# Prompt heads of a differential attention: five score banks, and the second sub-head turned by a diagonal and added in PSUM

## The chip, the cores and the metric

The kernel runs on one core of one Trainium2 chip. What is measured is the device time of one execution in microseconds (us), as the median of several runs.

## The reference

One inference step of four layers: 0 = gated short convolution, 1 = a gated linear recurrence, 2 = differential attention, 3 = the convolution again. All in fp32, width 1024. The layers work on a prompt of 1024 tokens and on a sample group of 8 sequences with 4 new tokens each, whose 2048 earlier keys and values lie in pages of 128 rows. The change touches the attention of the prompt, in layer 2. It has 8 heads, each with two sub-heads of 64 query and key columns and one value of 128 columns:

```python
def diff_combine(p, lam):
    p = p.reshape(p.shape[0], N_HEADS, 2, p.shape[2], p.shape[3])
    return p[:, :, 0] - lam * p[:, :, 1]

# diff_attn_prompt, for a block of 128 queries:
sc = jnp.einsum('bqhd,bkhd->bhqk', qi, k).astype(jnp.float32)
sc = jnp.where(kpos[None, :] <= qpos[:, None], sc, -jnp.inf)
w = diff_combine(jax.nn.softmax(sc, axis=-1), lam).astype(v.dtype)
return jnp.einsum('bhqk,bkhd->bqhd', w, v)

# diff_attn_output:
of = of * lax.rsqrt(jnp.mean(jnp.square(of), axis=-1, keepdims=True) + SUBLN_EPS)
return (o * jax.nn.silu(z)) @ w_out
```

So a head's output is the difference of two softmaxes times the values, divided by its root mean square over 128 columns, gated, and projected by w_out.

## The kernel before, in words

Layer 2 runs as follows. The projections for queries, keys, values and gate come first (`qkv`, `zpath`); beside them the sample group's keys are read page by page and scored (`sample_keys`). Then `heads` works through the prompt's attention, and beside it `sample_values` reads 128 pages of values, 512 KB each, on SP's queue into five buffers, and multiplies each page by the sample group's probabilities (tile sacc, line 1524). Behind both the output projection starts (`boundary`, tile op, line 127).

`heads` goes over 64 blocks, 8 heads by 8 query blocks; block qb has (qb + 1) * 128 keys. A block passes through these steps, spread over three rounds of the loop, so that three blocks (`cur`, `old`, `older`) are in work at once:

- `score`: for each of the two sub-heads one or two chunks of up to 512 keys, two matmuls each, into a PSUM bank (tile S, line 1210). DVE finds the minimum (lines 1248 and 1250; scores have their sign turned, and the last chunk takes the mask with it).
- `expo`: ACT reads the bank, writes the probabilities P of the sub-head to SBUF and their sum to rr (line 1262).
- `combine`: DVE adds the sums of the two chunks (line 1279), takes reciprocals (1281), forms the factor -lambda * sum0 / sum1 in a column of rr (1282), and writes P0 + factor * P1 over P0 (1284, one instruction over all keys of the block).
- `turn`: PE transposes P0 in pieces of 128x128 into a bank (tile wtp, line 1293), and ACT copies the bank to SBUF (tile wt, line 1295).
- `apply`: PE multiplies the turned pieces by the values (tile pv, line 1303).
- `finish`: ACT scales by 1 / sum0 into O (line 1312), then squares O and sums the squares (tile sq, line 1314). After every fourth block `outputs` (DVE line 1217, GpSimd lines 1218 and 1220) divides four blocks by their root mean square, and `store` transposes them (ytp, 1226) and gates them (1229 to 1232).

PSUM has eight banks. In this stage three of them (tag R) hold scores, one each (Q and U) serve turns, pv and ytp in turn, and three (P) serve the sample group: sacc, and in `gather_o` the transposes of its result (tile sot, line 1553). A tile of a tag waits until the tile that had its bank before was read.

`chain` ties the order of DVE's instructions for minima and combine to the written order. All other order is a planner's: the program is written as one list, the values' pieces merged into the heads' by the costs that the generators `yield`, with the total `tot` and a factor `ahead` of 1.1 (the values are to be done when the heads are at 1 / 1.1 of their cost); the heads' instructions get a priority of 50 places; and a simulation with its own durations decides the order on each engine. An engine then works strictly in that order.

Of the kernel before, what the change touches and what calls it, by code (L numbers as in the profile page):

```python
# [10 lines left out]
F32 = mybir.dt.float32  # L11
# [3 lines left out]
AF = mybir.ActivationFunctionType  # L15
ALU = mybir.AluOpType
AX = mybir.AxisListType
PSUM = bass.MemoryType.PSUM
# [28 lines left out]
class Trunk:  # L47
# [30 lines left out]

    def bank(self, kind, name):
        tag = next(self.deals[kind])  # L80
        pool = self.psb if tag in "PQ" else self.psum
        return pool.tile([128, 512], F32, tag=tag, bufs=self.BANKS[tag], name=name)

    def tp(self, name):
# [1086 lines left out]
    def heads(self, y):  # L1171
        nc = self.nc
        ident = self.ident
        lo_, hi_ = slice(0, 64), slice(64, 128)
        halves = ((lo_, hi_), (hi_, lo_))
        ks, V, sz, qs, O, ss = {}, {}, {}, {}, {}, {}
# [93 lines left out]
        def chain(inst):  # L1270
            if last:
                self.after(inst, last.pop())
            last.append(inst)

        def combine(x):
            qb, P, rr = x["qb"], x["P"], x["rr"]
            N = (qb + 1) * 128
            if N > 512:
                chain(nc.vector.tensor_reduce(
                    rr[:, 0:2], rr[:, 16:20].rearrange("p (s i) -> p s i", s=2), axis=AX.X, op=ALU.add))  # L1280
            chain(nc.vector.reciprocal(rr[:, 4:6], rr[:, 0:2]))
            chain(nc.vector.scalar_tensor_tensor(
                rr[:, 10:11], rr[:, 0:1], rr[:, 5:6], self.nlam, ALU.mult, ALU.mult))
            chain(nc.vector.scalar_tensor_tensor(
                P[0][:, :N], P[1][:, :N], rr[:, 10:11], P[0][:, :N], ALU.mult, ALU.add))

        def turn(x):
            h, qb, P = x["h"], x["qb"], x["P"]
            x["w"] = []
            for o, w in chunks(qb):  # L1290
                wp = self.tp(f"wtp{h}_{qb}_{o}")
                for j in range(0, w, 128):
                    nc.tensor.transpose(wp[:, j : j + 128], P[0][:, o + j : o + j + 128], ident)
                wt = self.pp.tile([128, 512], F32, tag="wt", bufs=self.n_wt, name=f"wt{h}_{qb}_{o}")
                nc.scalar.copy(wt[:, :w], wp[:, :w])  # L1295
                x["w"].append(wt)
# [9 lines left out]
        def finish(x):  # L1306
            h, qb = x["h"], x["qb"]
            g, qj = divmod(qb, 4)
            if qj == 0:
                O[0] = self.pp.tile([128, 4, 128], F32, tag="O", bufs=self.n_o, name=f"O{h}_{g}")  # L1310
                ss[0] = self.ropep.tile([128, 4], F32, tag="ss", bufs=2, name=f"ss{h}_{g}")
            nc.scalar.activation(O[0][:, qj], x["pv"], AF.Identity, scale=x["rr"][:, 4:5])
            sq = self.ropep.tile([128, 128], F32, tag="sq", bufs=1, name=f"sq{h}_{qb}")
            nc.scalar.activation(sq, O[0][:, qj], AF.Square, accum_out=ss[0][:, qj : qj + 1])

        def begin(h, qb):
            return dict(h=h, qb=qb, S={}, P=[], rr=self.ropep.tile(
# [11 lines left out]
        cur, old, older, out = begin(0, 0), None, None, []  # L1329
        score(cur, 0)  # L1330
        for nxt in blocks[1:] + [None, None, None]:
            if old:
                combine(old)
            if cur:
                h, qb = cur["h"], cur["qb"]
                expo(cur, 0)
                score(cur, 1)
                yield 220 * (qb + 1)
                if qb in (2, 5):
                    g = qb // 3  # L1340
                    sz[h, g] = self.pp.tile([128, 512], F32, tag="sz", bufs=self.n_sz, name=f"sz{h}_{g}")
                    nc.sync.dma_start(sz[h, g], self.zd[h][:, 512 * g : 512 * g + 512])
                if qb == 1:
                    queries(h, 1)
                    yield 430
                if h < 7 and qb in (4, 5):
                    keys(h + 1, qb - 4)
                    yield 430
                if h < 7 and qb == 6:
                    queries(h + 1, 0)  # L1350
                    yield 430
            if older:
                finish(older)
                if older["qb"] % 4 == 3:
                    out.append((older["h"], older["qb"] // 4, outputs(older["h"], older["qb"] // 4)))
            if old:
                turn(old)
                yield 110 * (old["qb"] + 1)
                apply(old)
                yield 216 * (old["qb"] + 1)  # L1360
            if cur:
                expo(cur, 1)
            new = begin(*nxt) if nxt else None
            if new:
                score(new, 0)
            if out and (not older or older["qb"] % 4 != 3 or not nxt):
                store(*out.pop(0))
                yield 430
            cur, old, older = new, cur, old
# [25 lines left out]
    def sample_keys(self):  # L1395
        nc = self.nc
# [3 lines left out]
        cw, wp = self.pool("psw", space=PSUM, reuse_waits="tile")  # L1400
        qb = kp.tile([128, 2, 4, 2, 2, 32], F32, name="qbd")
# [87 lines left out]
        turn(todo.pop())  # L1489
        cw.__exit__(None, None, None)  # L1490
        ck.__exit__(None, None, None)
        self.cpb, self.psb = self.pool("psb2", space=PSUM, reuse_waits="tile")


    def sample_values(self, y):
# [52 lines left out]

    def gather_o(self, b, os_):
        nc = self.nc  # L1550
        tp = self.tps(f"sot{b}")
        for e in range(2):
            nc.tensor.transpose(tp[:, 128 * e : 128 * e + 128], os_[:, 128 * e : 128 * e + 128], self.ident)
        ov = self.ots[:, :, NQ * b : NQ * b + NQ].rearrange("p (e g) m -> p g e m", e=2)
        for e in range(2):
            src = tp[:, 128 * e : 128 * e + 128].rearrange("p (g r) -> p g r", g=4)[:, :, 8 * e : 8 * e + 8]
            nc.vector.tensor_reduce(
                ov[:, :, e, :], src.rearrange("p g (s q) -> p g q s", s=2), axis=AX.X, op=ALU.add
            )

    def attn_layer(self, l, u):
        nc = self.nc


        def merge(main, total, side, cost):
            debt = 0.0
            for c in main:
                debt += c * cost / total
                while debt > 0:
                    n = next(side, -1)  # L1570
                    if n is None:
                        break
                    if n < 0:
                        debt = -1e18
                        break
                    debt -= n

        def rest(side):
            for _ in side:
                pass  # L1580

        cq, self.pq = self.pool("pq", reuse_waits="tile")
        self.deal(tp="U", tps="U", mm="R")
        keys = self.sample_keys()
        next(keys)
        g = self.qkv(u)
        next(g)
        merge(g, 47 * 5120.0, keys, self.shares[0] * KEY_COST)
        cq.__exit__(None, None, None)
        ct, self.tmp = self.pool("tmpq", reuse_waits="tile")  # L1590
        z, ztot = self.zpath(u), 8 * 10.2 * NT
        merge(itertools.islice(z, 20), ztot, keys, self.shares[1] * KEY_COST)

        cpa, self.ppa = self.pool("ppa", reuse_waits="tile")
        hs = self.heads(u)
        next(hs)
        merge(z, ztot, keys, self.shares[1] * KEY_COST)
        rest(keys)
        ca, self.pp = self.pool("pp", reuse_waits="tile")
        self.deal(tp="QU", tps="P", mm="R")  # L1600
        tot = 64 * 9 * 110.0 + 288 * 324.0 + 16 * 430
        values = self.sample_values(u)
        next(values)

        def main():
            while True:
                with self.tc.high_priority(50):
                    c = next(hs, None)
                if c is None:
                    break  # L1610
                yield c

        merge(main(), tot, values, VALUE_COST * self.ahead)
        rest(values)
        ca.__exit__(None, None, None)
        cpa.__exit__(None, None, None)
        ct.__exit__(None, None, None)

    def run(self):
        nc, tc, a = self.nc, self.tc, self.a  # L1620
# [47 lines left out]
        def trunk_bufs():  # L1668
            self.deal(tp="PPPQ", mm="RRRU")
            self.bufs = dict(sm=8, u=2, xat=6, xr=2, xn=3, xc=3)  # L1670
# [40 lines left out]
        if self.layers > 1:  # L1711
            ct.__exit__(None, None, None)
            bufs = self.bufs
# [5 lines left out]
            cs, sp = self.pool("smq", side="right")  # L1719
# [8 lines left out]
        if self.layers > 2:  # L1728
# [7 lines left out]
            self.attn_consts(cp)  # L1736

            self.attn_layer(2, A)
            for cm in (cr, cc, cs):
                cm.__exit__(None, None, None)  # L1740
            trunk_bufs()
            ca, self.tmpa = self.pool("tmp1a", reuse_waits="tile")
            cms, B = [ca], []
# [96 lines left out]
```

## Time and profile before

| | |
|---|---|
| median of 3 runs | 2407.99 us (2405.65 to 2415.18) |
| the profiled execution | 2409.33 us |
| its span, first to last instruction | 2407.7 us |
| PE busy in the span | 2277.3 us (95%) |
| PE weight loads busy | 1946.8 us (81%) |
| DVE busy | 1453.2 us (60%) |
| ACT busy | 929.2 us (39%) |
| GpSimd (POOL) busy | 337.1 us (14%) |
| bytes moved | 393.41 MB, 163 GB/s in the mean |

PE is TensorE's matmuls and PEld its weight loads, which run beside them; DVE is VectorE, ACT is ScalarE, POOL is GpSimd, SP issues most DMAs. The shares are means over the whole span, in which stages with different limits follow one another. Matmuls are pipelined, and a busy PE counts from the start of one to its modelled end, so that a stream of short ones can be closer together than their lengths. The heads run from about 1490 to 1848 us of the span.

### The profile page before, as it was taken

The page shows a single profiled execution, that of the slowest core. Times are in us where ns is not written, and L with a number is a line of the kernel's source. Part 1 is how long each engine was busy: PE and PEld are TensorE (multiplying, and loading weights), DVE is VectorE, ACT ScalarE, POOL GpSimd, SP SyncE. Part 2 cuts the span into 40 slices and gives each one's busy share as a digit, 9 for nine tenths or more (in the row PEclk, how much of TensorE's full clock was granted, in tenths as well). Part 3 has the DMA queues.
Part 4 walks back from the last instruction along what each step waited for, and adds up shares of the span by engine and source line. Part 5 has one row for each costly group of instructions (what it writes and reads, how often), then busy time and mean ns, then how long its engine had stood idle before and what let it go on. Part 6 is the DMA issues. An engine that isn't in the chain of part 4 may idle for free.

```text
span 2407.7 us, 45325 instructions
## 1 busy us (share of the span) xinstructions
PE 2277.3 (95%) x17288; PEld 1946.8 (81%) x17288; DVE 1453.2 (60%) x3015; ACT 929.2 (39%) x1906; POOL 337.1 (14%) x541
## 2 busy tenths in 40 slices
PE   7999999999999999988999998888888999999997
PEld 4989999997888886766666886555557999999997
DVE  6865655457456545656555554677675477666555
ACT  4333333346544423322221113667665243333410
POOL 0200000001001000233223322333220000000000
PEclk9999999999999999999999998999999999999999
DMA  9243344423444535768677766999993222222442
GB/s 329 77 145 111 91 121 150 133 82 120 139 131 124 154 108 171 217 201 255 222 242 253 244 189 203 277 298 291 281 299 116 84 85 62 68 59 70 128 131 76
DMA packets 289391, 393.41 MB, mean 163 GB/s; under 512 B 18749, under 2 KB 197054, under 8 KB 289174
## 3 DMA queue, kind: packets, MB, share of 16 engines
q1 hardware_dynamic: 247190, 306.61, 42.1%
q0 software_dynamic: 20480, 67.13, 9.1%
q10 hardware_dynamic: 21504, 16.78, 2.1%
q8 instruction: 136, 2.23, 0.4%
q14 instruction: 81, 0.66, 0.1%
HBM read 331.14 MB, written 59.31 MB: 162 GB/s over the span
## 4 chain that ended last, share of the span: by engine, by line
PE 64%; issue 13%; DMA 11%; POOLq 5%; POOL 2%; DVE 2%; ACT 1%; SPq 1%; DVEq 0%; ACTq 0%
PE op L127 15%; PE inX L612 12%; PE inZ L612 6%; DMA vp<-cache_v 6%; PE xb L127 4%; PE z L127 4%; POOLq L1381 4%; PE in L127 3%; PE inY L612 3%; PE ada L200 3%; PE in L733 2%; PE in L648 2%; PE g L903 2%; POOL kp L1388 2%; PE sacc L1524 1%
## 5 line engine op out<-in xcount | busy, mean ns | idle before, releaser
L1099 PE MATMUL qk<-wq,ua 128*128 128x512 f32 x1152 | 284.1, 401 | 8.7 <-DVE wq L1067 5.5
L1099 PEld LDWEIGHTS qk<-wq,ua 128*128 128x128 f32 x1152 | 213.2, 189 | 68.4 <-DVE wq L1067 8.1
L1476 DVE STREAM_TRANSPOSE kt<-kp 128x512 f32<-128x512 f32 x256 | 172.0, 697 | 138.5 <-DMA kp<-cache_k 107.1
L1388 POOL DMA_DIRECT2D kp<-cache_k x256 | 137.9, 539 | 336.1 <-DVE kt L1476 188.8
L294 DVE SCALAR_TENSOR_TENSOR r<-op,gate,xr 128x384 f32<-128x384 f32 (+1 forms) x96 | 54.2, 570 | 127.4 <-PE op L127 82.5
L1262 ACT ACTIVATE P<-S,rr 128x512 f32<-128x512 f32 (+2 forms) x192 | 110.8, 583 | 47.1 <-DVE rr L1250 31.5
L1210 PE MATMUL S<-ks,qhl 128*128 128x512 f32 (+2 forms) x384 | 110.8, 395 | 13.8 <-ACT P L1262 7.4
L127 PE MATMUL zz<-ua,wz 128*128 128x384 f32 (+1 forms) x576 | 99.0, 331 | 7.0 <-DVE zt L1165 7.0
L1210 PEld LDWEIGHTS S<-ks,qhl 128*128 128x128 f32 x384 | 60.8, 196 | 54.8 <-ACT P L1262 30.7
L127 PEld LDWEIGHTS zz<-ua,wz 128*128 128x128 f32 x576 | 95.6, 193 | 11.4 <-DVE zt L1165 7.8
L127 PEld LDWEIGHTS z<-ub,wrz 128*128 128x128 f32 x576 | 92.6, 188 | 11.7 <-issue 10.1
L1524 PE MATMUL sacc<-vp,pv 128*16 128x256 f32 x1024 | 80.3, 389 | 22.9 <-DMA vp<-cache_v 22.7
L127 PE MATMUL z<-ub,wrz 128*128 128x384 f32 (+1 forms) x576 | 98.2, 326 | 0.0
L1303 PEld LDWEIGHTS pv<-V,wt 128*128 128x128 f32 x576 | 73.7, 194 | 22.5 <-ACT wt L1295 13.4
L127 PEld LDWEIGHTS xb<-ub,wrx 128*128 128x128 f32 x504 | 80.9, 188 | 12.7 <-issue 9.2
L1420 PE MATMUL sps<-kt,qbd 32*32 32x512 f32 x2048 | 78.8, 621 | 11.9 <-DVE kt L1476 11.9
L331 POOL TENSOR_TENSOR rs<-mv,mhalf 128x1 f32<-128x1 f32 (+1 forms) x36 | 19.1, 541 | 504.3 <-DVE mv L329 497.6
L127 PE MATMUL op<-ua,ub 128*128 128x384 f32 (+1 forms) x504 | 89.7, 333 | 0.0
L127 PEld LDWEIGHTS op<-ua,ub 128*128 128x128 f32 x504 | 81.9, 192 | 9.1 <-issue 9.0
L127 PE MATMUL xb<-ub,wrx 128*128 128x384 f32 (+1 forms) x504 | 87.9, 328 | 0.0
L1303 PE MATMUL pv<-V,wt 128*128 128x128 f32 x576 | 82.3, 284 | 5.8 <-ACT wt L1295 5.3
L200 PE MATMUL ada<-wada,ct 128*32 128x512 f32 x384 | 82.7, 616 | 4.1 <-DMA wada<-w_ada 2.9
(492 smaller groups left out, 5112.4 us busy)
## 6 DMA issues: line engine op xcount, KB each, us to landing
kp<-cache_k POOLq DMA_DIRECT2D x256, 256.0 KB, 3.8
vp<-cache_v SPq DMA_DIRECT2D x128, 512.0 KB, 10.0
wada<-w_ada SPq DMA_DIRECT2D x96, 512.0 KB, 4.2
xa<-xat SPq DMA_DIRECT2D x64, 192.0 KB, 2.6
wra<-a_w_in SPq DMA_DIRECT2D x24, 512.0 KB, 4.1
wrb<-a_w_in SPq DMA_DIRECT2D x24, 512.0 KB, 4.1
xr<-xa SPq DMA_DIRECT2D x64, 192.0 KB, 2.5
tok<-kd SPq DMA_DIRECT2D x32, 256.0 KB, 7.0
```

Of the source, the lines that this page charges most:

```text
L127: nc.tensor.matmul(ps[:, :n], wt[:, wp, k], self.ucols(units[k], up, c), start=i == 0, stop=i == 3 * KB - 1)
L200: nc.tensor.matmul(ps[c : c + 32, :], self.ct[:, k], wts[k // 2][:, k % 2], start=k < 4, stop=k >= 4, tile_position=(0, c),)
L612: nc.tensor.matmul(B[tgt][jj][:, :QH], w[n][:, wp, k], mov[k](jj, up), start=new and m == 0, stop=m == 11, skip_group_check=not new)
L1099: nc.tensor.matmul(ps, u[k][:, c0 : c0 + 128], wq[n, k // 2][:, wp, k % 2], start=i == 0, stop=i == 3 * KB - 1)
L1210: nc.tensor.matmul(st[:, o : o + w], qs[h, g][:, part, s, 128 * qj : 128 * qj + 128], ks[h][:, s, l0 : l0 + w], start=part == 0, stop=part ...
L1262: nc.scalar.activation(p[:, o : o + w], x["S"][s][i][:, :w], AF.Exp, scale=-1.0, bias=rr[:, 6 + s : 7 + s], accum_out=rr[:, c : c + 1])
L1303: nc.tensor.matmul(x["pv"], x["w"][kb // 4][:, j : j + 128], V[h][:, kb], start=kb == 0, stop=kb == qb)
L1381: ld, (r,) = nc.values_load_multi_w_load_instructions(self.ptab[0:1, idx : idx + 1], engines=[et], min_val=0, max_val=159)
L1388: d = eng.dma_start(t, a[src].rearrange(pat)[bass.ds(r, 1), :, cs].rearrange("a p f -> p (a f)"))
L1420: nc.tensor.matmul(ps[b][32 * g : 32 * g + 32, r], qf[rows, f, g, k], kt[rows, g, k], start=f == 0 and k == 0, stop=f == 1 and k == 3, til ...
L1476: nc.vector.transpose(ktv[:, :, j], ring.pop(0).rearrange("p (f t) -> p f t", t=32))
L1524: nc.tensor.matmul(acc[32 * g : 32 * g + 16, :], pt[:k, j, g], vv[:k, :, g], start=j == 0, stop=j == NPG, tile_position=(0, 32 * g))
```

## The change

- `score` gets five banks: R keeps three, two more (tag V) are dealt out with them, and the sample group keeps one bank (P) for sacc. sot goes to the banks Q and U.
- `combine` no longer touches P. It writes a 128x128 matrix d, the identity times the factor of each row (DVE tensor_scalar).
- `turn` uses plain matmuls for each 128x128 piece, P0 against the identity and P1 against d, both into the same PSUM columns, the second adding to the first.
- `finish` squares and sums O on DVE (tensor_tensor_reduce with an accumulator) where ACT did it.
- The costs that the merge counts for `turn` and in `tot` are raised, the deal of banks is set where the banks are opened, and after the stage the bank pool is closed and opened again with the earlier sizes.

```diff
-        pool = self.psb if tag in "PQ" else self.psum
+        pool = self.psb if tag in "PQV" else self.psum
...
         def combine(x):
-            qb, P, rr = x["qb"], x["P"], x["rr"]
-            N = (qb + 1) * 128
-            if N > 512:
+            qb, rr = x["qb"], x["rr"]
+            if qb > 3:
...
-            chain(nc.vector.scalar_tensor_tensor(
-                P[0][:, :N], P[1][:, :N], rr[:, 10:11], P[0][:, :N], ALU.mult, ALU.add))
+            x["d"] = d = self.ropep.tile([128, 128], F32, tag="dg", bufs=2, name=f"dg{x['h']}_{qb}")
+            chain(nc.vector.tensor_scalar(d, ident, rr[:, 10:11], None, ALU.mult))
...
                 for j in range(0, w, 128):
-                    nc.tensor.transpose(wp[:, j : j + 128], P[0][:, o + j : o + j + 128], ident)
+                    for s, r in enumerate((ident, x["d"])):
+                        nc.tensor.matmul(
+                            wp[:, j : j + 128], P[s][:, o + j : o + j + 128], r, start=s == 0, stop=s == 1)
...
-            nc.scalar.activation(sq, O[0][:, qj], AF.Square, accum_out=ss[0][:, qj : qj + 1])
+            nc.vector.tensor_tensor_reduce(
+                sq, O[0][:, qj], O[0][:, qj], scale=1.0, scalar=0.0, op0=ALU.mult, op1=ALU.add,
+                accum_out=ss[0][:, qj : qj + 1])
...
                 turn(old)
-                yield 110 * (old["qb"] + 1)
+                yield 220 * (old["qb"] + 1)
...
+        self.BANKS = dict(self.BANKS, P=1, V=2)
         self.cpb, self.psb = self.pool("psb2", space=PSUM, reuse_waits="tile")
+        self.deal(tp="QU", tps="P", mm="RRRVV")
...
-        tp = self.tps(f"sot{b}")
+        tp = self.tp(f"sot{b}")
...
-        self.deal(tp="QU", tps="P", mm="R")
-        tot = 64 * 9 * 110.0 + 288 * 324.0 + 16 * 430
+        tot = 64 * 9 * 110.0 + 288 * 434.0 + 16 * 430
...
-            for cm in (cr, cc, cs):
+            for cm in (cr, cc, cs, self.cpb):
                 cm.__exit__(None, None, None)
+            self.BANKS = dict(self.BANKS, P=3)
+            self.cpb, self.psb = self.pool("psb3", space=PSUM, reuse_waits="tile")
```

## Rows read from the trace of the kernel before

**Rows 1.** Busy us by stretch: PE, PEld, DVE, ACT, POOL, granted clock, DMA share, GB/s.

```profile
1500.00:1812.00 312.00, 269.11 (x2247) 171.93 (x2247) 224.56 (x578) 210.27 (x648) 93.89 (x66) 0.98 1.02 291
1812.00:1848.00 36.00, 27.98 (x191) 23.06 (x190) 21.95 (x55) 21.93 (x62) 4.09 (x4) 0.98 0.18 57
```

**Rows 2.** DMA, 1500 to 1812 us: packets; issues with KB each, us to landing.

```profile
DMA packets 37839, 90.69 MB, mean 291 GB/s; under 512 B 3559, under 2 KB 12775, under 8 KB 37802
...
vp<-cache_v SPq DMA_DIRECT2D x123, 512.0 KB, 10.1
```

**Rows 3.** Chain of waits, 1500 to 1812 us, shares by line.

```profile
by line: DMA vp<-cache_v 45.6%; PE sacc L1524 9.3%; PE S L1210 7.8%; DMA tok<-qd 6.9%; PE pv L1303 5.9%; PE wtp L1293 3.2%; issue 2.6%; DMA tok<-kd 2.2%; DVE P L1284 2.0%; DVE os L1530 1.7%; ACT P L1262 1.6%; DVE rr L1282 1.1%; PE ytp L1226
```

**Rows 4.** Waits on PE and PEld, 1500 to 1812 us: total us, times, longest.

```profile
PE sacc L1524 <- DMA vp<-cache_v: 22.7, 27, 1.9
PE wtp L1293 <- DVE P L1284: 7.1, 7, 1.8
PE S L1210 <- ACT P L1262: 6.0, 9, 1.6
...
PEld sacc L1524 <- DMA vp<-cache_v: 33.4, 34, 2.3
PEld S L1210 <- ACT P L1262: 21.6, 41, 1.8
```

**Rows 5.** Groups by line, 1500 to 1812 us: busy, mean ns | idle before.

```profile
L1293 PE MATMUL wtp<-ident,P 128*128 128x128 f32 x259 | 41.8, 284 | 7.6 <-DVE P L1284 7.1 <-ACT wt L1295 0.3
```

**Rows 6.** Timeline, streams of turns and of pv: start, us from first to last end.

```profile
1814.27 0.60 PE L1293 MATMUL wtp<-ident,P 128*128 128x128 f32 x4
...
1820.94 1.60 PE L1303 MATMUL pv<-V,wt 128*128 128x128 f32 x12 [0.46 <-ACT wt L1295]
...
1838.48 1.03 PE L1293 MATMUL wtp<-ident,P 128*128 128x128 f32 x8
...
1839.76 2.05 PE L1303 MATMUL pv<-V,wt 128*128 128x128 f32 x16 [0.24 <-ACT wt L1295]
```

**Rows 7.** Groups by line, 1500 to 1812 us, DVE and ACT.

```profile
L1284 DVE SCALAR_TENSOR_TENSOR P<-P,rr,P 128x512 f32<-128x512 f32 (+7 forms) x58 | 54.2, 935 | 1.8
...
L1282 DVE SCALAR_TENSOR_TENSOR rr<-rr,nlam 128x1 f32<-128x1 f32 x58 | 21.5, 371 | 2.0
...
L1314 ACT ACTIVATE sq<-O 128x128 f32<-128x128 f32 x57 | 18.0, 316 | 0.9
...
L1250 DVE DVE_READ_ACCUMULATOR2_ANT rr<- 128x1 f32 x115 | 16.1, 140 | 0.0
...
L1314 ACT ACTIVATION_READ_ACCUMULATOR sq<-O 128x1 f32 x57 | 11.2, 197 | 0.0
...
L1217 DVE TENSOR_SCALAR ss<-ss 128x4 f32<-128x4 f32 x14 | 5.2, 370 | 4.0 <-ACT sq L1314 3.9
```

**Rows 8.** Groups by line and shape, 1500 to 1848 us, DVE: the smallest minimum.

```profile
L1250 DVE CUSTOM_DVE_ANT_0 S<-S,cmask 128x128 f32<-128x128 f32 x14 | 4.4, 311 | 0.0
```

**Rows 9.** Timeline, where one sample batch ends and the next starts.

```profile
1702.25 1.97 DVE L1530 TENSOR_SCALAR os<-sacc,coef 16x256 f32<-16x256 f32 x4 [1.99 <-PE sacc L1524]
...
1704.64 1.06 PE L1524 MATMUL sacc<-vp,pv 128*16 128x256 f32 x16
```

**Rows 10.** Timeline of the last block's turn: what runs before it.

```profile
1834.16 4.48 PE L127 MATMUL op<-ua,wo 128*128 128x384 f32 x24 [0.65 <-ACT P L1262]
...
1835.73 1.28 DVE L1284 SCALAR_TENSOR_TENSOR P<-P,rr,P 128x1024 f32<-128x1024 f32 x1
```

**Rows 11.** Instructions of tile P: durations in ns, minimum, median, maximum.

```profile
L1284 DVE SCALAR_TENSOR_TENSOR P<-P,rr,P x64: 343/884/2930, 1494.4 to 1835.7; 128x128 f32<-128x128 f32 x8, 128x256 f32<-128x256 f32 x8, 128x384 f32<-128x384 f32 x8, 128x512 f32<-128x512 f32 x8
```

**Rows 12.** Groups of PE by line, 1812 to 1848 us.

```profile
L1303 PE MATMUL pv<-V,wt 128*128 128x128 f32 x60 | 8.0, 280 | 1.0 <-ACT wt L1295 1.0
L1210 PE MATMUL S<-ks,qhl 128*128 128x512 f32 (+2 forms) x18 | 5.9, 415 | 1.1 <-ACT P L1262 1.1
L1293 PE MATMUL wtp<-ident,P 128*128 128x128 f32 x27 | 4.0, 274 | 0.4 <-DVE P L1284 0.4
```

## The prediction, made before the changed kernel was run

> **What bounds the kernel now.** I read the page's busy shares first, then the busy time of each engine by stretch, then the DMA queues, the chain of waits and the waits of TensorE inside the stretch that the change touches. The change lies in the prompt heads, which run beside the sample values from about 1490 to 1848 us. In 1500 to 1812 us PE is busy for 269.11 of 312 us, DVE for 224.56 and ACT for 210.27, while the DMA share is 1.02 at 291 GB/s [rows 1]: the 16 transfer engines never pause. 90.69 MB pass there, 123 of the 128 value pages among them, each 10.1 us from issue to landing [rows 2]. The chain of waits in that stretch is led by those pages, with 45.6%, and only then come lines of PE [rows 3]. So the end of the stretch is set by transfers, which the change doesn't touch. Behind it, in 1812 to 1848 us, the DMA share is 0.18, and the last head blocks run out on the engines [rows 1].
>
> TensorE is second in line, and how far behind decides the case. Its sacc matmuls stand idle for pages for 22.7 us by the matmul rows and 33.4 us by the weight-load rows [rows 4]. That is the cover for any work added to PE. A busy 269 us doesn't mean that PE runs at its peak: 259 turns count as 41.8 us, 0.161 us each [rows 5], but in one stream a further turn costs (1.03 - 0.60)/4 = 0.108 us [rows 6].
>
> **The change part by part.** *The turn.* 288 transposes become 576 fp32 matmuls of the same shape. Their nearest row is pv, also fp32 on 128x128 weights and 128 moving columns: (2.05 - 1.60)/4 = 0.113 us for each further one [rows 6]. In 1500 to 1812 us there are 259 turns [rows 5]: 518 x 0.113 - 259 x 0.108 = 30.6 us more of PE. Outside it there are 29: 3.4 us.
>
> *The combine.* 58 instructions over both probabilities leave DVE in the stretch, 54.2 us [rows 7]. A diagonal of 128x128 replaces each. It has no row; below it costs nothing, above it is 0.37 us, the mean of the one-column instruction in front of it, and I take 0.31 us, as the 128x128 row of the minima [rows 7, 8]: 18 us. PE's wait for the combined P, 7.1 us [rows 4], should mostly go; what is late next is the diagonal, about 0.6 us earlier than the mean 0.94 us combine would have ended.
>
> *The sums of squares.* ACT loses 18.0 us of Square and 11.2 us of its accumulator reads [rows 7]. DVE gains, per block, what the 128x128 minimum and its accumulator read cost: 0.311 + 0.140 = 0.45 us [rows 7, 8], 26 us for 57. DVE's net is -54 + 18 + 26 = -10 us, ACT's -29 us; both are under 75% busy, so as work this is worth nothing. As a wait it may matter: DVE now waits in its queue for O, which comes from ACT behind pv; behind that instruction stand the minima, for which the exponentials on ACT wait, and for those the scores' banks. Today DVE waits for ACT's sum of squares only in L1217, 3.9 us before 14 instructions, 0.28 us each [rows 7]. For 57 that is 16 us; the other end is 0, where the written order puts it after O is ready. I take 0, as DVE keeps 312 - 225 = 87 us of slack in the stretch [rows 1], and keep 16 us for a rival.
>
> *Five score banks.* PE's scores wait for ACT to read a bank: 6.0 us by the matmul rows, 21.6 us by the weight loads [rows 4]. With two more banks this may go whole or not at all (minima are chained, ACT reads in order). I take the lower row, 6 us.
>
> *One bank for the sample sums, and their gather in the heads' banks.* A batch's first sacc must now wait until DVE has read the last batch's sums. Before, the next batch already starts only after that: DVE reads the sums from 1702.25 to 1704.22, the next sacc starts at 1704.64 [rows 9]. So 0 for the seven changes of batch; at the other end, where DVE's read is late by its own length, 7 x 1.97 = 14 us of PE, which pages in flight would cover in part. Behind a waiting sacc on PE stand scores and turns, and on SP's queue the issue of the page five further on. The gather's two transposes take a bank of the turns eight times; same ends, with 8 for 7. No transfer is added or moved, and the values keep their share of the emission order, since the total grows with the turns' cost. The pool opened anew at the end reuses banks that scores and sums have left: 0.
>
> **The sum.** In 1500 to 1812 us PE has 22.7 to 33.4 us of waiting for pages, is given 30.6, and gets back 7.1 + 6.0 = 13 us: it still has 5 to 16 us to spare, and pages end the stretch as before: 0. Without anything given back it lacks up to 8 us. Since work and transfers don't line up page by page, I take +2 us. In the tail 29 turns cost 3.4 us, of which those of the last two blocks, 15 x 0.113 = 1.7 us, stand on the path. The last combine gives nothing back: P is ready at 1835.73 + 1.28 = 1837.01, and PE comes to the turn at 1838.48, because 24 matmuls of the output projection stand in front of it until 1838.6 [rows 6, 10]. The last sum of squares changes engine at about equal price (0.316 us before its read on ACT, 0.311 on DVE [rows 7, 8]). So +2 us there. The profiled execution took 2409.33 us, 1.62 us over its span and 1.34 us over the median of 2407.99; with +4 us, and one taken off for the median, I forecast 2412 us, +0.17%: no change. A measurement of this kernel can tell about 0.5%, 12 us, from none.
>
> **The rivals.** *Slower: DVE waits for O.* Place: the sum of squares at the head of DVE's queue, with the next minima behind it. Price: up to 16 us by L1217's row, and as much again if the two inputs from SBUF are held up by GpSimd, as the combine was (0.88 us in the median, 2.93 us at worst [rows 11]; 64 such instructions go and 64 come, but now in front of the minima). It decides once PE's spare 5 to 16 us are gone, so above some 0.2 us for a block. Time: 2412 + 32 - 10 = 2434 us. For it: O itself comes late, behind turn, copy and pv of the same block, and each minimum behind it holds up an exponential. Against it: DVE has slack, and 3.9 us is little.
>
> The Trainium skill, "SBUF — State Buffer", "Who interferes with whom", says that a DVE instruction with two SBUF inputs, or one in a two-port mode such as tensor_scalar can enter, shuts out or is shut out by a GpSimd instruction reading SBUF for that one's whole length. The worst combine agrees; whether the diagonal is held as well no row shows, and by that rule this rival would gain 64 more places to wait in.
>
> *Faster: the heads run ahead.* With five banks and no long combine, the order on PE may place the heads' last blocks before the last pages. After 1812 us pv, scores and turns are busy for 8.0 + 5.9 + 4.0 = 18 us [rows 12]; if all of it moved forward, 2412 - 18 = 2394 us, and it decides from about 16 us on, nine tenths of it. For it: the scores' wait for a bank is what holds the heads back on PE [rows 4]. Against it: the heads' emission is still tied to the values by the same ratio of 1.1, and most of PE's cover before 1812 us goes into the added turns.
>
> *No spare banks in effect.* The minima are chained on DVE, so scores that are early only wait. Then 7 us come back, not 13, and the stretch ends 0 to 1 us later, up to 8 us with the combine's wait kept too: 2411 to 2418 us, still no change.
>
> *A matmul dearer than a transpose.* If each of the 576 took four times a turn's 0.108 us, PE would get 576 x 0.43 - 288 x 0.108 = 217 us, some 180 us beyond its cover: about 2590 us. The pv row at 0.113 us for the very same types and shape speaks against it. The Trainium skill, "TensorE: Matmul & The Clock Gate", "Terms", calls transposing mode four times faster for fp32, which would give this time; pv and the turns, 0.113 to 0.108 us, don't agree with it.
>
> **How the numbers follow.** Forecast 0.50, no spare banks 0.14, DVE waits 0.22, heads ahead 0.13, dearer matmul 0.01. Faster by over 0.5% (under 2396 us) is the heads' case alone, 0.13 with those that come out a little less but find other savings; slower by over 0.5% (over 2420 us) is DVE's wait, the dear matmul, and a twentieth of the forecast's part where one bank for sums costs its 14 us: 0.25; the rest, 0.62, is the same. The range runs from the heads' case to DVE's wait, 2396 to 2434 us; the forecast's own is 2405 to 2420 us.
>
> **What would show it.** Right: the DMA share stays at about 1.0 and falls off within 5 us of 1812; the waits of sacc for pages shrink to 5 to 15 us; turns are 576 with a slope of 0.11 us; PE busy in the stretch is some 290 to 300 us; DVE is some 10 us lower. Wrong: a DMA share under 0.97 in the stretch, waits of scores or turns that grow where those for pages vanish, minima or exponentials waiting for the sum of squares, or head blocks that are all done before the last page.

## The result, and the profile after

The changed kernel took 2492.21 us (2487.97 to 2493.67, 4 runs) beside 2411.31 us for the kernel before; the ratio is 1.0335, with an interval of 1.0306 to 1.0363. It is 81 us slower, and the forecast was +4 us with a range that ended at 2434 us. The profiled execution took 2487.97 us.

The head of the page gives the size of it. The columns are busy us, share of the span and the number of instructions; the first line is of the kernel before, the rest of the changed one:

```profile
PE 2277.3 (95%) x17288; PEld 1946.8 (81%) x17288; DVE 1453.2 (60%) x3015; ACT 929.2 (39%) x1906; POOL 337.1 (14%) x541
...
span 2486.0 us, 47172 instructions
## 1 busy us (share of the span) xinstructions
PE 2377.9 (96%) x18152; PEld 2047.9 (82%) x18152; DVE 1430.6 (58%) x3143; ACT 907.4 (36%) x1778; POOL 336.8 (14%) x541
```

PE is busy for 2377.9 - 2277.3 = 100.6 us more and the span is 78.3 us longer. PE runs 18152 - 17288 = 864 more matmul instructions. The forecast had counted 576 in place of 288, so 288 more. 864 is 1152 - 288, and the groups by line say the same (1490 to 1926 us, the stretch of the heads; busy, mean ns | idle before):

```profile
L1295 PE MATMUL wtp<-ident,P 128*128 128x128 f32 x576 | 114.1, 280 | 7.2 <-ACT P L1262 6.0 <-DVE yt L1229 0.9 <-ACT O L1315 0.2
L1295 PE MATMUL wtp<-dg,P 128*128 128x128 f32 x576 | 111.8, 276 | 0.0
...
L1306 PE MATMUL pv<-V,wt 128*128 128x128 f32 x576 | 82.6, 281 | 1.3 <-ACT wt L1298 1.3
```

The loop writes 288 matmuls against the identity and 288 against the diagonal; the chip ran 576 of each. The same holds for pv: its loop writes one for each of the 288 pieces, as many as there were transposes, and the row counts 576. A written fp32 matmul of this tile ran as two PE instructions; a transpose ran as one (288 in all before, 259 of them in [rows 5]). The kernel before had both counts (count, then shortest, median and longest in ns, first and last start; the count at a line's end is of a sample):

```profile
L1293 PE MATMUL wtp<-ident,P x288: 270/273/444, 1495.2 to 1839.2; 128*128 128x128 f32 x144
...
L1303 PE MATMUL pv<-V,wt x576: 270/275/579, 1497.6 to 1841.5; 128*128 128x128 f32 x192
```

The timeline of the changed kernel shows the pairs and their price (start, us to the end of the last, x in the stream):

```profile
1821.55 0.38 PE L1295 MATMUL wtp<-ident,P 128*128 128x128 f32 x2
1821.77 0.39 PE L1295 MATMUL wtp<-dg,P 128*128 128x128 f32 x2
1822.00 0.39 PE L1295 MATMUL wtp<-ident,P 128*128 128x128 f32 x2
1822.22 0.39 PE L1295 MATMUL wtp<-dg,P 128*128 128x128 f32 x2
1822.44 0.39 PE L1295 MATMUL wtp<-ident,P 128*128 128x128 f32 x2
```

From start to start a matmul takes (1822.44 - 1821.55)/4 = 0.223 us, two instructions of 0.111 us. A piece of 128 keys now costs 0.445 us of PE where its transpose cost 0.108 us [rows 6]: 288 x (0.445 - 0.108) = 97 us, which is the growth of PE's busy time but for 4 us.

The stretches (columns as in [rows 1]):

```profile
1500.00:1812.00 312.00, 293.72 (x2569) 205.38 (x2570) 162.21 (x549) 147.54 (x409) 75.01 (x53) 0.99 0.91 280
1812.00:1926.00 114.00, 101.77 (x748) 92.40 (x746) 63.06 (x226) 66.70 (x186) 22.43 (x17) 0.99 0.19 56
```

Up to 1812 us PE is now at 294 of 312 us and the DMA share falls from 1.02 to 0.91: the transfers pause. Behind 1812 us there are 114 us of heads where there were 36. The DMA view and the chain of waits of 1500 to 1812 us, for [rows 2, 3]:

```profile
DMA packets 32760, 87.49 MB, mean 280 GB/s; under 512 B 3399, under 2 KB 8560, under 8 KB 32722
...
vp<-cache_v SPq DMA_DIRECT2D x125, 512.0 KB, 7.3
```

```profile
by line: DMA vp<-cache_v 31.8%; PE wtp L1295 15.9%; PE sacc L1531 14.8%; PE S L1210 13.3%; PE pv L1306 8.9%; DMA tok<-kd 4.1%; issue 2.5%; POOL ks L1198 1.7%; SPq L1183 1.5%; ACT ks L1195 1.3%; SPq L1386 1.0%; ACT P L1262 0.9%; SPq L1393 0.
```

A page lands after 7.3 us, not 10.1, at a DMA share of 0.91 where it was 1.02; the turn, 3.2% of the chain before, is 15.9% of it. The waits of PE in the same stretch, for [rows 4]:

```profile
PE sacc L1531 <- DMA vp<-cache_v: 16.9, 14, 3.2
...
PEld sacc L1531 <- DMA vp<-cache_v: 20.0, 17, 2.6
...
PEld S L1210 <- ACT P L1262: 8.1, 19, 0.5
```

Waits for pages have shrunk by 6 to 13 us, no more; the scores' wait for a bank has fallen from 21.6 to 8.1 us, and the turn's wait for the combined P (7.1 us) is gone. Over the whole stretch of the heads (columns as in [rows 1], the kernel before first) PE stood idle for 53.6 us before and for 36.6 us after:

```profile
1490.00:1848.00 358.00, 304.39 (x2464) 200.09 (x2464) 253.84 (x659) 238.38 (x729) 100.53 (x72) 0.97 0.93 268
...
1490.00:1926.00 436.00, 399.45 (x3325) 300.73 (x3324) 230.26 (x786) 217.69 (x602) 102.30 (x73) 0.99 0.72 222
```

Three of PE's waits over these stretches add up to that difference, and the others nearly cancel. The three are the waits for pages, 22.7 us before and 16.9 after; for the combine, 7.5 us and none; and for the copy of the turned pieces, 5.3 us and 1.3. The last two are shown here, the line after the dots from the changed kernel:

```profile
PE wtp L1293 <- DVE P L1284: 7.5, 8, 1.8
PE pv L1303 <- ACT wt L1295: 5.3, 13, 0.8
...
PE pv L1306 <- ACT wt L1298: 1.3, 2, 1.1
```

The new DVE instructions over the heads' stretch, for [rows 7, 8]:

```profile
L1317 DVE CUSTOM_DVE_ANT_0 sq<-O 128x128 f32<-128x128 f32 x64 | 28.3, 442 | 35.1 <-ACT O L1315 34.7
...
L1284 DVE TENSOR_SCALAR dg<-ident,rr 128x128 f32<-128x128 f32 x64 | 18.3, 286 | 3.7
...
L1317 DVE DVE_READ_ACCUMULATOR2_ANT ss<- 128x1 f32 x64 | 5.2, 81 | 0.0
```

The diagonal costs 0.286 us (0.31 was taken), the sum of squares 0.442 + 0.081 = 0.52 us (0.45 was taken). The mean of the sum of squares hides two cases (shortest, median and longest in ns):

```profile
L1317 DVE CUSTOM_DVE_ANT_0 sq<-O x64: 273/290/2350, 1502.7 to 1921.2; 128x128 f32<-128x128 f32 x64
```

Ten of the 64 took 0.51 to 2.35 us, and the timeline has a GpSimd instruction of line 1198, 1204 or 1220 running beside each of the ten.

### The profile page after: what moved, and what is told of

Same layout as the page of the kernel before. It is cut to its first block, busy times and chain, and to the rows that moved or that the text cites. A ratio compares the mean times of both kernels' runs of the same rounds, so it can differ in the third digit from the quotient of the medians.

```text
span 2486.0 us, 47172 instructions
## 1 busy us (share of the span) xinstructions
PE 2377.9 (96%) x18152; PEld 2047.9 (82%) x18152; DVE 1430.6 (58%) x3143; ACT 907.4 (36%) x1778; POOL 336.8 (14%) x541
## 4 chain that ended last, share of the span: by engine, by line
PE 67%; issue 14%; DMA 8%; POOLq 4%; POOL 3%; ACT 2%; DVE 1%; SPq 1%; DVEq 0%; ACTq 0%
PE op L127 14%; PE inX L612 11%; PE inZ L612 6%; DMA vp<-cache_v 4%; PE xb L127 4%; PE z L127 4%; PE in L127 4%; POOLq L1386 4%; PE inY L612 3%; PE wtp L1295 3%; PE ada L200 2%; PE S L1210 2%; PE in L733 2%; PE in L648 2%; PE sacc L1531 2%
## 5 line engine op out<-in xcount | busy, mean ns | idle before, releaser
L1295 PE MATMUL wtp<-ident,P 128*128 128x128 f32 x576 | 114.1, 280 | 7.2 <-ACT P L1262 6.0
L1295 PE MATMUL wtp<-dg,P 128*128 128x128 f32 x576 | 111.8, 276 | 0.0
L1295 PEld LDWEIGHTS wtp<-ident,P 128*128 128x128 f32 x576 | 89.0, 192 | 16.9 <-issue 6.4
L127 PEld LDWEIGHTS z<-ub,wrz 128*128 128x128 f32 x576 | 92.6, 188 | 11.7 <-issue 10.1
L1531 PE MATMUL sacc<-vp,pv 128*16 128x256 f32 x1024 | 85.3, 383 | 17.7 <-DMA vp<-cache_v 16.9
L1295 PEld LDWEIGHTS wtp<-dg,P 128*128 128x128 f32 x576 | 87.8, 193 | 0.7 <-DVE dg L1284 0.7
```

Source lines behind the costliest of these rows:

```text
L127: nc.tensor.matmul(ps[:, :n], wt[:, wp, k], self.ucols(units[k], up, c), start=i == 0, stop=i == 3 * KB - 1)
L1295: nc.tensor.matmul(wp[:, j : j + 128], P[s][:, o + j : o + j + 128], r, start=s == 0, stop=s == 1)
L1531: nc.tensor.matmul(acc[32 * g : 32 * g + 16, :], pt[:k, j, g], vv[:k, :, g], start=j == 0, stop=j == NPG, tile_position=(0, 32 * g))
```

## The experiments

Theory A: the second instruction of each fp32 matmul is the loss. Its rivals: the banks and the sum of squares on DVE, the order in which pages and heads stand, and reading both probabilities with the addition in PSUM. Each comparison is with the kernel before on the same chip: 2405.62 us for the turn alone, the rest alone, half of the turn and the pages spread further; 2407.72 us for the turn in one pass, the banks, the squares and the four banks; 2409.07 us for the two runs without pages.

**The turn alone**, put into the kernel before with its diagonal and its merge costs; banks and squares stay as they were.

```diff
...
-            chain(nc.vector.scalar_tensor_tensor(
-                P[0][:, :N], P[1][:, :N], rr[:, 10:11], P[0][:, :N], ALU.mult, ALU.add))
+            x["d"] = d = self.ropep.tile([128, 128], F32, tag="dg", bufs=2, name=f"dg{x['h']}_{qb}")
+            chain(nc.vector.tensor_scalar(d, ident, rr[:, 10:11], None, ALU.mult))
...
-                    nc.tensor.transpose(wp[:, j : j + 128], P[0][:, o + j : o + j + 128], ident)
+                    for s, r in enumerate((ident, x["d"])):
+                        nc.tensor.matmul(
+                            wp[:, j : j + 128], P[s][:, o + j : o + j + 128], r, start=s == 0, stop=s == 1)
...
```

> The kernel before with the new combine and turn alone: three score banks, sums of squares on ACT. Theory A (price of the turn): an fp32 matmul is two PE instructions of 0.112 us where a transpose is one of 0.109, so the turn costs 1152 x 0.112 - 288 x 0.109 = 98 us of PE instead of the 34 us forecast; some 15 to 25 us of it lie in waits for pages, so this kernel takes about 2480 to 2500 us, as the whole change. Theory B (DVE waits for O, or the banks): the turn costs the 34 us forecast and is mostly hidden, about 2410 to 2425 us. Theory C (five banks help the turn): 2500 us or more.

Measured 2488.8 us, ratio 1.0352 (1.033 to 1.0374): the whole loss. PE is busy for 2377.9 us and runs 18152 matmul instructions, both as in the changed kernel. Theory A holds, and the five banks do not change the time of the new turn. Nor are they what shortened the scores' wait for a bank: with three banks it is shorter still in 1500 to 1812 us, 3.6 us by the weight loads where the changed kernel has 8.1:

```profile
PE S L1210 <- ACT P L1262: 0.5, 2, 0.3
...
PEld S L1210 <- ACT P L1262: 3.6, 8, 0.6
```

**The rest alone**: the changed kernel with the old combine, the transposing turn and the old merge costs (the edit of the turn is shown).

```diff
...
-                    for s, r in enumerate((ident, x["d"])):
-                        nc.tensor.matmul(
-                            wp[:, j : j + 128], P[s][:, o + j : o + j + 128], r, start=s == 0, stop=s == 1)
+                    nc.tensor.transpose(wp[:, j : j + 128], P[0][:, o + j : o + j + 128], ident)
...
```

> The changed kernel with the combine and the transposing turn of before, and its merge costs: five score banks, one bank for sample sums, sums of squares on DVE remain. Theory A: within 12 us of before, 2396 to 2420 us. Theory B (DVE's queue is held by the sum of squares, or one bank holds up the pages): at least half of the loss is here, 2450 us or more.

Measured 2416.87 us, ratio 1.0038 (1.002 to 1.0057). It is within the bound of theory A, but 9 us on the slow side; the two runs on the parts below follow from that.

**Half of the turn**: the changed kernel with the identity's matmul alone.

```diff
-                    for s, r in enumerate((ident, x["d"])):
-                        nc.tensor.matmul(
-                            wp[:, j : j + 128], P[s][:, o + j : o + j + 128], r, start=s == 0, stop=s == 1)
+                    nc.tensor.matmul(
+                        wp[:, j : j + 128], P[0][:, o + j : o + j + 128], ident, start=True, stop=True)
```

> The changed kernel with the first matmul of each turn alone (the identity; the second sub-head is left out of the result, its factor and diagonal are still made). Theory A: 576 PE instructions of 0.112 us for 288 transposes of 0.109: 33 us of PE more than before, which waits for pages mostly cover: 2405 to 2425 us. Theory B (a matmul costs as a transpose): no more PE than before, 2400 us; PE busy over the whole span tells the two apart: 2277 + 33 = 2310 us by A, 2277 by B. If the loss comes from DVE or the banks: 2450 us or more.

Measured 2412.42 us, ratio 1.0028 (1.0014 to 1.0042). The turn's group in the profile, one matmul written for each of 288 pieces:

```profile
L1294 PE MATMUL wtp<-ident,P 128*128 128x128 f32 x576 | 85.2, 285 | 10.1 <-ACT P L1262 6.4 <-DVE ots L1563 1.9 <-ACT O L1314 0.9
```

Each is two instructions again. PE is busy for 2303.1 us in all, 26 us more than before (A: 33, B: 0), and the time is 7 us longer. The rest alone, which has no added matmul, is as slow, so none of the 26 us need have reached the end. This kernel has the added work that the forecast had reckoned for the whole change (576 instructions for 288), and its time is close to the forecast time. It keeps the raised merge costs of the change, so those are not the loss.

**The turn in one pass**: the changed kernel with P, the identity and the diagonal rounded to fp32r, a rounded form of fp32. Both sub-heads and the addition in PSUM stay.

```diff
-            p = self.pp.tile([128, T], F32, tag="P", bufs=self.n_p, name=f"P{h}_{qb}_{s}")
+            p = self.pp.tile([128, T], F32R, tag="P", bufs=self.n_p, name=f"P{h}_{qb}_{s}")
...
-            x["d"] = d = self.ropep.tile([128, 128], F32, tag="dg", bufs=2, name=f"dg{x['h']}_{qb}")
+            x["d"] = d = self.ropep.tile([128, 128], F32R, tag="dg", bufs=2, name=f"dg{x['h']}_{qb}")
...
-                    for s, r in enumerate((ident, x["d"])):
+                    for s, r in enumerate((self.identr, x["d"])):
```

> The changed kernel with probabilities, identity and diagonal rounded to fp32r, so that each turn matmul is one PE instruction and not two; both sub-heads, the diagonal and the accumulation in PSUM stay. Theory A (the loss is the second pass of each fp32 matmul, 0.112 us): 576 x 0.112 - 288 x 0.109 = 33 us more PE work than before, mostly covered, 2405 to 2425 us. Theory D (the loss comes from reading both probabilities or from adding in PSUM, whatever a matmul costs): 2480 us or more. If an fp32r matmul of 128 columns takes as long as the two passes, also 2480 us, and the slope of the turns in the timeline is 0.22 us.

Measured 2430.45 us, ratio 1.0097 (1.0063 to 1.0131): 23 us of the 81 remain. The groups and a stream from the timeline:

```profile
L1297 PE MATMUL wtp<-identr,P 128*128 128x128 f32 x288 | 71.2, 281 | 6.8 <-ACT P L1264 6.4 <-DVE yt L1231 0.4
L1297 PE MATMUL wtp<-dg,P 128*128 128x128 f32 x288 | 69.4, 277 | 0.2 <-DVE dg L1286 0.2
```

```profile
1702.78 0.27 PE L1297 MATMUL wtp<-identr,P 128*128 128x128 f32 x1
1702.89 0.28 PE L1297 MATMUL wtp<-dg,P 128*128 128x128 f32 x1
1703.00 0.28 PE L1297 MATMUL wtp<-identr,P 128*128 128x128 f32 x1
```

288 instructions for 288 matmuls, one each 0.11 us. Theory D falls: same data, same additions, a third of the added PE work (2308.8 us busy, +31.5), under a third of the loss. The time is 5 us over the range of theory A. It is some 16 us more, by ratios 0.7%, than the half turn with equally many instructions; there P1 and the diagonal were not read. What makes these 16 us was not tried and stays open; in 1490 to 1866 us of the two, the scores' weight loads wait for ACT to read a bank for 25.2 us here and for 7.6 us there.

**Pages spread further**: the changed kernel with the factor ahead at 0.75.

```diff
-            self.shares, self.ahead, self.n_vp = (0.76, 0.26), 1.1, 5
+            self.shares, self.ahead, self.n_vp = (0.76, 0.26), 0.75, 5
```

> The changed kernel with the factor ahead at 0.75 for 1.1, so that in PE's written order 70 of 576 turn matmuls stand behind the last page where there are 196. Theory A1 (all of the loss is PE work): the work stays, the tail shrinks and the stretch with the pages grows by as much: 2480 to 2495 us. Theory A2 (part of the loss is that the pages are done too early, with PE waiting for them in front and heads alone behind): PE need in the stage is some 335 of 436 us, and spreading the pages wins 15 to 40 us: 2450 to 2475 us.

Measured 2491.19 us, ratio 1.0359 (1.034 to 1.0378), as theory A1 has it. The last sums of a page now start at 1872 us instead of 1806 us, and the transfers pause much of the time:

```profile
L1531 PE MATMUL sacc<-vp,pv x1024: 376/379/610, 1496.7 to 1871.7; 128*16 128x256 f32 x171
...
1700.00:1750.00 50.00, 46.34 (x398) 35.02 (x397) 28.43 (x96) 25.33 (x70) 12.27 (x10) 1.00 0.73 231
1750.00:1800.00 50.00, 44.64 (x353) 36.55 (x354) 27.86 (x95) 25.37 (x73) 12.73 (x10) 0.97 0.57 168
```

So the long tail of the changed kernel is not a loss by order. Moving pages into it only moves the heads forward. With the new turn PE, at 45 to 46 of 50 us, sets most of the time in either order.

**The parts of the rest.** Five banks alone, and squares on DVE alone, each in the kernel before (the main lines of both edits):

```diff
...
+        self.BANKS = dict(self.BANKS, P=1, V=2)
...
+        self.deal(tp="QU", tps="P", mm="RRRVV")
...
-        tp = self.tps(f"sot{b}")
+        tp = self.tp(f"sot{b}")
```

> The kernel before with five score banks and one bank for the sample sums, their gather in the heads' banks, and nothing else of the change. The run without the new turn took 0.38% more than before (some 9 us). Theory G (the gather in the heads' banks and the single bank cost it): this one is slower by the same 4 to 12 us, 2410 to 2418 us, with PE waiting for some 8 us in front of the gather's transposes. Theory Q (the sum of squares in DVE's queue costs it): this one is at the level of before or up to 6 us under it, 2400 to 2408 us.

```diff
-            nc.scalar.activation(sq, O[0][:, qj], AF.Square, accum_out=ss[0][:, qj : qj + 1])
+            nc.vector.tensor_tensor_reduce(
+                sq, O[0][:, qj], O[0][:, qj], scale=1.0, scalar=0.0, op0=ALU.mult, op1=ALU.add,
+                accum_out=ss[0][:, qj : qj + 1])
```

> The kernel before with the sums of squares on DVE and nothing else of the change. Theory G: within 3 us of before, 2403 to 2409 us. Theory Q: 4 to 12 us more, 2410 to 2418 us, with DVE's waits for O longer than its waits for the sum of squares were before.

Banks: 2417.55 us, ratio 1.004 (1.0019 to 1.0061), in the range of theory G. Its profile has PE waiting before the gather, in 1490 to 1850 us, and the scores waiting for a bank:

```profile
PE S L1210 <- ACT P L1262: 16.3, 15, 6.4
PE sot L1557 <- DVE os L1534: 7.6, 6, 2.1
```

The wait before the gather was 0.7 us before. But the profiled execution took 2408.16 us, the second fastest of twelve and no slower than the kernel before, so it does not show that this wait is the loss. The scores' wait, 7.4 us in the kernel before, did not fall with five banks alone. Squares: 2412.16 us, ratio 1.0017 (1.0 to 1.0034): at most a small loss, but in theory Q's range and not in G's. So the two runs put most of the 9 us on the banks, by ratios 0.4% against 0.2%, and do not exclude a part from the squares. DVE waits for O as the rival said, and little comes of it:

```profile
DVE sq L1314 <- ACT O L1312: 19.9, 15, 3.5
```

**Four banks**: the kernel before with one more score bank, and two left to the sample sums and their gather.

```diff
...
+        self.BANKS = dict(self.BANKS, P=2, V=1)
...
+        self.deal(tp="QU", tps="P", mm="RRRV")
```

> The kernel before with four score banks, two banks left to the sample sums and their gather (so the gather is not in the heads' banks), old combine, old turn, squares on ACT. In PE's written order no score, no turn and 4 of 288 products with values stand behind the last page, where before 12 of 384, 22 and 26 did. If pages bound the stretch and PE's need of some 243 us leaves room beside them, the tail behind the last page goes: 12 to 20 us less than before, 2386 to 2394 us. If the heads in front of the last page only delay the pages, as in the run with ahead at 0.75, the time stays within 6 us of before.

Measured 2398.92 us beside 2407.72, ratio 0.9961 (0.9944 to 0.9978): 9 us faster than the kernel before, though less than hoped. The gather waits 2.8 us for DVE, and no score and no turn is left behind the last page. The DMA share in 1500 to 1812 us is 1.02 as before:

```profile
1500.00:1812.00 312.00, 273.93 (x2307) 180.93 (x2305) 236.72 (x615) 221.89 (x695) 97.37 (x68) 0.98 1.02 289
```

But the last sums of a page start later, at 1823.9 us here and at 1815.4 us in the kernel before (here, then before):

```profile
L1528 PE MATMUL sacc<-vp,pv x1024: 379/379/634, 1501.1 to 1823.9; 128*16 128x256 f32 x171
...
L1524 PE MATMUL sacc<-vp,pv x1024: 379/379/634, 1499.1 to 1815.4; 128*16 128x256 f32 x171
```

So the tail goes, as the expectation said, and the pages come 8 us later. That this delay is the part of the gain that is missing was not tried.

**Without pages**: before and after, with five pages read and used for all.

```diff
+        kept = [self.page("cache_v", j, f"vp0_{j}", self.n_vp) for j in range(5)]
...
-                v = self.page("cache_v", b * NPG + j, f"vp{b}_{j}", self.n_vp) if j < NPG else vs
+                v = kept[(b * NPG + j) % 5] if j < NPG else vs
```

> The kernel before without 123 of its 128 value pages: five are read once and used for all (the sample values in the result are left out in that sense; all matmuls stay). Theory P (pages set the end of the stretch before, and TensorE has about 30 us of cover under them): 25 to 45 us less than before, 2362 to 2382 us. Theory W (PE's written order and its own waits set it, pages seldom come last): under 12 us less.

> The changed kernel without 123 of its 128 value pages, as in the run beside it. Theory P (with 97 us more matmul work PE sets the end itself and the cover is used up): 5 to 20 us less than the changed kernel, 2470 to 2487 us, clearly less than the pages are worth before. If waits for pages still cost the changed kernel what its rows say (29 us in front of sacc): 25 to 35 us less, 2457 to 2467 us. Between the two kernels without pages the turn costs its whole price then: 75 to 100 us more for this one by either.

Before without pages: 2425.97 us, ratio 1.0078 (1.0049 to 1.0108), slower, which neither theory allowed. After without pages: 2474.99 us, ratio 1.0275 (1.0244 to 1.0305), some 15 us under the changed kernel. The second lies in the range of theory P, and the 15 us are close to the 16.9 us that PE waits for pages in the changed kernel. That fits these waits still costing there what the matmul rows say, though the order changed as well. The first was not a clean removal. With no page to wait for, the planner put the sample sums far in front, and then the heads ran alone:

```profile
1600.00:1650.00 50.00, 50.00 (x517) 27.55 (x506) 33.25 (x83) 27.50 (x85) 12.65 (x10) 1.00 0.24 66
...
1700.00:1750.00 50.00, 36.80 (x210) 29.52 (x208) 38.25 (x100) 37.10 (x116) 18.78 (x14) 0.93 0.33 90
```

Heads with the old turn keep PE busy for 37 of 50 us when nothing stands beside them; their scores wait 32.2 us for ACT over the stretch. The turn's price between these two kernels is 49 us and not 75 to 100; these rows suggest that here it fills gaps of the heads' own. How much the pages alone held back the kernel before can't be read from these runs.

## Why the prediction was wrong, step by step

- *The turn: the step that failed.* "288 transposes become 576 fp32 matmuls of the same shape. Their nearest row is pv": the row was the right one, its slope of 0.113 us was right, and it was the slope of one instruction, of which pv has two for each matmul. The row's own count says so, 576 for 288 pieces (the sum of qb + 1 over 64 blocks), against 288 for the turns on the same pieces; in [rows 6] the last block, of eight pieces, has x8 turns beside x16 products. 30.6 + 3.4 = 34 us should have been 97 us. The runs with the turn alone, with half of it and with it in one pass show that this term is the loss. One sign of being right came true by luck: PE is busy for 293.72 us in 1500 to 1812 us, as forecast, because the rest of the added work moved behind 1812 us. The sign of being wrong, a DMA share under 0.97, is the one that told.
- *A matmul dearer than a transpose.* This rival had the right mechanism, with a chance of 0.01 and a factor of four, and was set aside by the same misread row. The factor is 0.223 / 0.108 = 2.06. The Trainium skill, "TensorE: Matmul & The Clock Gate", "Terms", has four; this trace agrees with its direction and not with its size, and the text should not have said that the pv row speaks against a dearer matmul.
- *The cover.* 5 to 16 us were to be left after 34 us of new work, out of 22.7 to 33.4 us of waits for pages and 13 us given back. Of the 100.6 us that PE got, 100.6 - 78.3 = 22 us don't show in the span, 17 us of them in the heads' stretch. Waits for pages gave only 6 us there (22.7 to 16.9 us); the combine gave 7.5 us and the copy of the turned pieces 4 us. So most of the waits for pages were not cover: 97 us of new work left 16.9 us of them standing. That the 22 us come near to the 22.7 us of [rows 4] is chance. Even with 97 us and the whole cover as reckoned, 36 to 46 us, the sum would have come to some 2460 to 2470 us, still below the result: the cover, too, was taken too large.
- *Pages set the end of the stretch.* The DMA share fits this before (1.02) and for the half turn (1.00), but no run shows it for the kernel before, as the one meant to was not a clean removal. With the whole turn the share is 0.91, and the run with ahead at 0.75 shows PE setting most of the time.
- *Combine and five banks.* The waits they were to remove did shrink in the changed kernel, 7.1 us to none and 21.6 us to 8.1 us [rows 4]. The second is not the banks' work: it falls to 3.6 us with the new turn and three banks, and five banks alone leave it. As time they gave nothing: banks alone cost 0.4%.
- *One bank for the sums, gather in the heads' banks.* Taken at 0 with 14 to 16 us as the other end; the banks' run puts it, together with the five score banks, at some 10 us. A wait of 7.6 us was seen in front of the gather, in an execution that was no slower than the kernel before, so the cause of the 10 us stays open. The gather and the single bank were not tried apart there; the run with four banks changes both.
- *DVE waits for O.* The wait came: 34.7 us in the changed kernel, where L1217's row had given 16 us and the rival, with a hold-up by GpSimd, 32 us. The hold-up came as well: ten long sums of squares, each beside a GpSimd instruction, against a median of 0.290 us. The diagonal took at most 0.290 us in the changed kernel; with the turn alone seven of the 64 took 0.76 to 1.38 us, each beside a GpSimd instruction. None of this decided: the turn alone, with squares on ACT, is as slow.
- *Heads ahead of the pages.* The opposite came in the changed kernel: 392 of the 1152 turn instructions stand behind the last page, 22 of 288 before. With four banks no turn was left there, and the kernel was faster by half of the 18 us.

## What to carry to other kernels

Before a row prices a new instruction, divide its count by the number of times that the program writes it: an operation that the chip runs as two instructions shows half its price in the slope. A transpose by matmul and a plain fp32 matmul of the same tile are not the same instruction, so folding an addition into a transpose can cost more on TensorE than the vector instruction it saves. An engine's waits for a transfer are not all cover for new work: here 97 us more of it took 6 of TensorE's 22.7 us of waits for pages, and 78 of the 100.6 us that it was busy longer came out as time.

## What the runs showed of the hardware that had not been expected

- A written fp32 matmul with 128x128 weights and 128 moving columns took two instructions, 0.223 us in a stream; the fp32 transpose of the same tile one, 0.108 us; the matmul of fp32r operands one, 0.11 us.
- The sum of squares took 0.290 us in the median, 0.442 us in the mean, and its accumulator read 0.081 us. Its ten long instances, 0.51 to 2.35 us, all ran beside a GpSimd instruction.
